# The first mixer of a two-layer encoder: values and gates follow each block, half of the output projection stands beside the last block's decays, and pools and load order are laid out anew

## The chip, the cores and the metric

One core of a Trainium2 chip runs the whole program: one launch, fp32 inputs and output in HBM. The metric is device microseconds of an execution, as a median over runs.

## The reference, cut to what matters

The program is an encoder trunk of two layers on 256 tokens of width 1024. Each layer is a token mixer and then a mixture of experts (MoE), each followed by a LayerNorm. The change touches the first mixer alone, and the order in which buffers are given to the MoE behind it.

```
q, f_fwd, f_bwd, v, gate = split(x @ w_in, 5)            # w_in 1024 x 5120
o = gated recurrence over time, forward and backward, 8 heads of 128
o = o * rsqrt(mean(o*o) + eps) * norm_w                   # by head
mix = (o * silu(gate)) @ w_out                            # w_out 1024 x 1024
x = LayerNorm(ALPHA * x + mix)
...
# MoE: top group of 4, its top 2 of 8 experts by token; 32 experts
hg, hu = split(xb @ w_up[e], 2);  y = (silu(hg) * hu) @ w_down[e]
```

All 32 experts' weights are read in both layers: 24 loads of 1 MB for a group of four experts, eight groups, 192 MB for a layer.

## The kernel before

**Weights.** Every weight comes in loads of 1 MB (`load`, line 87), issued on SyncE's (SP's) queue in the order of the program. A load is written to a slot of a ring. In the first mixer the ring is `ring1` with 9 slots (R1). For the first MoE there are 21 slots: the 9 of `ring1`, 4 of `ring2`, 5 of `ring3`, 3 of `ring4`. The last three lie in SBUF that the first mixer's own pools held. `MOE0_SLOTS` (line 34) is the order in which the first 21 loads of the MoE take slots, by ring number; it repeats after that. A load waits on SP until the last reader of what lay in its slot is done, and all loads behind it wait with it.

**Precision.** A weight is split in two fp32r parts, `whi` (ScalarE, line 265) and `wlo` (VectorE, line 266), a quarter of a load (128x512) at a time. A projection's quarter is 12 matmuls of 256 columns (`proj_w`, `proj_x`, lines 317 to 319 and 334 to 336); a quarter of the output projection is 6 matmuls of 512 columns (`out_proj`, lines 376 to 378). `Quarters` splits four quarters ahead of use.

**The first mixer, `hgrn`.** The 8 heads are four blocks b of two heads. For each block, `project(b)` (12 quarters) gives queries and forget gates; `decay(b)` makes the block's score matrix `am` in a first step (line 517) and eight levels (lines 546 and 532), each of which needs the products `kk` (line 563) and `qq` (line 566) of the level before from VectorE; `mix(b)` multiplies `am` by the values `vv` (line 594), normalises and multiplies by the gate `og`; `gate_turn(b)` (line 644) turns the result for the output projection. `values(c)` and `gated(c)` are projections of 4 quarters each. A `Side` weaves the nine steps of `decay(b)` into a stage's main work: `stage(b, quarters, main)` takes about 9 steps in that many quarters. Four stages follow `project(0)`. Then the output projection has its 16 quarters, with `mix(2)`, `mix(3)` and the preparation of the router (`routes`) between them.

**PSUM.** The levels of a decay use four banks with the tag `oa`, projections two with the tag `pj`. The output projection holds all four `oa` banks.

**The MoE.** LayerNorm statistics, the router and a gather come first; then for each group 16 loads of `w_up` (line 927) and 8 of `w_down`. The group's loads are issued as slots come free. Between the layers' MoEs stands a second mixer, a short convolution (`conv`).

Of the kernel before, what the change touches and what calls it, by code (L numbers as in the profile page):

```python
# [9 lines left out]
F32 = mybir.dt.float32  # L10
# [7 lines left out]
P = 128  # L18
D = 1024
# [11 lines left out]
FAR = 4096.0  # L31
RMS_EPS = 1e-6

MOE0_SLOTS = (2, 2, 2, 2, 1, 1, 4, 4, 4, 1, 1, 1, 3, 1, 3, 1, 1, 1, 3, 3, 3)
R1 = 9
R2 = 4
R3 = 5
# [4 lines left out]
def kernel(  # L42
# [31 lines left out]
    def bank(tag, bufs=2):  # L74
        return psum.tile([P, 512], F32, name=tag, tag=tag, bufs=bufs)
# [267 lines left out]
    def chain(*gens):  # L343
        for g in gens:
            yield from g
# [76 lines left out]
    def pools(left, name, n):  # L422
        return [left.enter_context(tc.tile_pool(name=f"{name}{k}", bufs=2, reuse_waits="tile")) for k in range(n)]
# [3 lines left out]

    def hgrn(src, left):
        w_in = hg_w_in[0]
        vam = left.enter_context(tc.tile_pool(name="vam", bufs=1))  # L430
        pm, px, pw, pj, pl = pools(left, "hg", 5)
        xtl = [p.tile([P, KD, T], F32R, name=n, bufs=1) for p, n in ((px, "xt"), (pl, "xl"))]
        rec = ExitStack()
        rc = rec.enter_context(tc.tile_pool(name="rec", bufs=2, side="right"))

        def x_evac(k2, v):
            ks = slice(2 * k2, 2 * k2 + 2)
# [2 lines left out]
        def qf(b):  # L440
            return [cols(w_in, D * z + 256 * b) for z in range(3)]

        vs = [cols(w_in, 3 * D + 256 * c) for c in range(4)]
        gs = [cols(w_in, 4 * D + 256 * c) for c in range(4)]
        order = qf(0) + vs[0:2] + qf(1) + vs[2:4] + qf(2) + gs[0:1] + qf(3) + gs[1:4]
        order += [rows(hg_w_out[0], 256 * c) for c in range(4)]
        ws = Quarters(pw, order, (0, 2, 1, 3), first=True, ahead=0,
                      between=lambda: load_x(1), lo_on=(0, 0, 0, 0))

        vv = vam.tile([P, NT, D], F32, name="vv")  # L450
        kmask = rc.tile([P, len(KINDS), P], U8, name="kmask", bufs=1)
        og = xb

# [8 lines left out]
        def project(b):  # L462
            ps = bank("pj")
            yield from proj_w(ps, xtl, ws)
            qq = rc.tile([P, 2, 2, T], F32, name="qq")
            kk = rc.tile([P, 2, 2, T], F32, name="kk")
            tt = rc.tile([P, 2, 2, T], F32, name="tt")
            QK[b] = qq, kk, tt
            th = pj.tile([P, 512], F32, name="th")
            act.activation(th, ps, AF.Tanh, scale=0.5)  # L470
            q0 = qq[:, 0].rearrange("p h t -> p (h t)")
            dve.scalar_tensor_tensor(q0, th, 1.0, ps, ALU.add, ALU.mult)
            for d in range(2):
                ps = bank("pj")
                yield from proj_w(ps, xtl, ws)
                th = pj.tile([P, 512], F32, name="th")
                act.activation(th, ps, AF.Tanh, scale=0.5)
                for h in range(2):
                    later.append((kk[:, d, h], tt[:, 1 - d, h], th[:, h * T:(h + 1) * T], 8 * d + 2 * b + h))

        ams = {}

        def firsts(kk, h):

# [7 lines left out]
        def decay(b):  # L492
            qq, kk, tt = QK[b]
            while later:
                forget()
            am = vam.tile([P, 2, NT, T], F32, name="am", bufs=4)
            ams[b] = am
            dst = am.rearrange("p hd j (k i) -> p hd j k i", k=2)

            def diag(rows_, cs):  # L500
                base = am[rows_, 0, 0, cs]
                return bass.AP(tensor=base.tensor, offset=base.offset,
                               ap=[base.ap[0], [NT * T, 2], [T + P, NT], list(base.ap[-1])])

            def scores(ps, kv):
                for hd in range(2):
                    for j in range(NT):
                        o = (hd * NT + j) * P
                        js = slice(j * P, (j + 1) * P)
                        yield ps[:, o:o + P], kv[:, hd, js], hd, js  # L510


            ks = rc.tile([P, 2, T], F32, name="ks", bufs=1)
            dve.tensor_tensor(ks, kk[:, 0], kk[:, 1], ALU.add)
            ps = bank("oa", 4)
            for o, kx, hd, js in scores(ps, ks):
                pe.matmul(o, kx, qq[:, 0, hd, js], start=True, stop=True)
            act.copy(diag(slice(0, P), slice(0, P)), ps.rearrange("p (hd j i) -> p hd j i", hd=2, j=NT))

            dve.tensor_tensor(qq[:, 1], qq[:, 0], tt[:, 1], ALU.mult)  # L520
            dve.tensor_tensor(qq[:, 0], qq[:, 0], tt[:, 0], ALU.mult)
            kc = firsts(kk, 1)
            yield

            tcur = tt
            for h in (1, 2, 4, 8, 16, 32, 64, 128):
                ps = bank("oa", 4)
                v = ps.rearrange("p (hd j i) -> p hd j i", hd=2, j=NT)
                if h == 128:
                    for hd in range(2):  # L530
                        for j in range(NT):
                            pe.matmul(v[:, hd, j], kk[:, j, hd, j * P:j * P + P],
                                      qq[:, 1 - j, hd, (1 - j) * P:(1 - j) * P + P], start=True, stop=True)
                    for j in range(NT):
                        act.copy(dst[:, :, j, 1 - j], v[:, :, j])
                    return


                def both(a, hd, o):
                    base = a[:, 0, hd, o:o + 1]  # L540
                    return bass.AP(tensor=base.tensor, offset=base.offset,
                                   ap=[base.ap[0], [2 * h, (P if hd is not None else 4 * P) // (2 * h)],
                                       [2 * T + h, 2], [1, h]])

                for o, kx, hd, js in scores(ps, kc):
                    pe.matmul(o, kx, both(qq, hd, js.start), start=True, stop=True)

                nb = T // (2 * h)

                def diagonal(a):  # L550

                    base = a[:, 0, 0, 0:1]
                    return bass.AP(tensor=base.tensor, offset=base.offset,
                                   ap=[base.ap[0], [2 * T + h, 2], [2 * h, 2 * nb], [1, h]])

                def factors(d):

                    base = tcur[:, 0, 0, 0:1]
                    o, step = (1, 4 * nb - 1) if d else (4 * nb + 1, -4 * nb - 1)
                    return bass.AP(tensor=base.tensor, offset=base.offset + o,  # L560
                                   ap=[base.ap[0], [step, 2], [2, 2 * nb], [0, h]])

                dve.tensor_tensor(diagonal(kk), diagonal(kk), factors(0), ALU.mult)
                if h < 64:
                    kc = firsts(kk, 2 * h)
                dve.tensor_tensor(diagonal(qq), diagonal(qq), factors(1), ALU.mult)
                if h < 64:
                    tn = rc.tile([P, 2, 2, nb], F32, name=f"tt{2 * h}", bufs=1)
                    tf = tcur.rearrange("p d hd (n s) -> p (d hd n) s", s=2)
                    pool.tensor_tensor(tn.rearrange("p d hd n -> p (d hd n)"), tf[:, :, 0], tf[:, :, 1], ALU.mult)  # L570
                    tcur = tn
                if h == 64:
                    for s in range(2):
                        r = slice(s * 64, s * 64 + 64)
                        act.copy(diag(r, slice(64 - s * 64, P - s * 64)), v[r, :, :, 64 - s * 64:P - s * 64])
                else:
                    dve.copy_predicated(diag(slice(0, P), slice(0, P)),
                                        kmask[:, KINDS.index(h), None, None, :].to_broadcast([P, 2, NT, P]), v)
                yield
# [95 lines left out]
            side.weave(main, after)  # L675
            side.finish()

        stage(0, 20, chain(values(0), values(1), project(1)))
        norms = load_norms()
        load_router(0)  # L680
        stage(1, 20, chain(values(2), values(3), project(2)))
        turn_norms(norms)
        stage(2, 16, chain(gated(0), project(3)), go_on((0, 6)))
        routes = router(0, lambda: pj.tile([P, 512], F32, name="th"))
        stage(3, 12, chain(gated(1), gated(2), gated(3)), go_on((1, 4), (2, 9)))
        rec.close()

        oa = [[bank("oa", 4) for f in range(2)] for t in range(NT)]
        for c in range(3):
            for _ in out_proj(oa, c, *m[c], ws):  # L690
                next(mixes[2], None)
                next(mixes[3], None)
                if c:
                    next(routes, None)
        run(routes)
        return finish_mixer(xb, src, oa, out_proj(oa, 3, *m[3], ws))

# [418 lines left out]
```

## Time and profile before

| what | value |
|---|---|
| time, median of 3 runs | 1241.23 us (1240.2 to 1242.97) |
| the profiled execution, own time | 1240.37 us |
| its span | 1238.6 us |
| busy: PE, VectorE, ScalarE, GpSimd | 976.2, 351.6, 268.1, 86.1 us |
| read from HBM | 447.05 MB |
| mean granted TensorE clock | 0.953 |

The span is the time from the first to the last instruction of the profiled execution; its own time is 1.77 us longer. A busy PE is one that has a matmul in its pipeline. The clock is a share of full speed, so 1.0 is 2.4 GHz and 0.5 is 1.2 GHz. All times inside the span count from its start.

### The profile page before, as it was taken

The numbers are of one execution on the slowest core, as the hardware profiler recorded it, in microseconds if no ns is written. First come the engines' busy times: TensorE is split into PE (matmuls) and PEld (weight loads), VectorE is DVE, ScalarE is ACT, GpSimd is POOL, SyncE is SP. The second block draws the span as 40 slices with busy tenths as digits, with TensorE's granted clock in tenths as the row PEclk, the third lists the DMA queues.
The fourth block names the chain that finished last, engine by engine and source line by source line (L and its number), as shares of the span: only waits on it lengthen the run. The fifth ranks groups of instructions, "written<-read, shape, count | busy, mean of one in ns | idle before, by whom it ended". The sixth has DMA issues, their size and how long they took to land. (4 is left out here: it accounts for less than half of the span.)

```text
span 1238.6 us, 15265 instructions
## 1 busy us (share of the span) xinstructions
PE 976.2 (79%) x6196; PEld 506.4 (41%) x6196; DVE 351.6 (28%) x602; ACT 268.1 (22%) x527; POOL 86.1 (7%) x98
## 2 busy tenths in 40 slices
PE   9999899787767676767678999879858767676875
PEld 8899897331213121222223999423213212121221
DVE  5767786310101111010103766331010101010103
ACT  5566543110101010100102554201101101010011
POOL 0110110000000000000000664000000000000001
PEclk9999999898998899998999999979998999999888
DMA  9733019999999999999999995999999999999994
GB/s 340 257 126 135 1 49 418 382 418 417 420 418 417 420 419 420 419 419 420 419 418 390 385 389 184 398 401 417 421 418 417 420 419 420 418 418 421 419 418 180
DMA packets 148304, 449.23 MB, mean 363 GB/s; under 512 B 11653, under 2 KB 44670, under 8 KB 148222
## 3 DMA queue, kind: packets, MB, share of 16 engines
q1 hardware_dynamic: 147884, 447.06, 90.5%
q8 instruction: 52, 0.85, 0.3%
q10 hardware_dynamic: 338, 1.07, 0.2%
q14 instruction: 30, 0.25, 0.1%
HBM read 447.05 MB, written 1.05 MB: 362 GB/s over the span
## 5 line engine op out<-in xcount | busy, mean ns | idle before, releaser
L927 PE MATMUL pj<-w,xg 128*32 128x512 f32 x2048 | 322.4, 629 | 92.3 <-DMA w<-in_moe_w_up_dram 92.3
L927 PE MATMUL oa<-w,hT 128*32 128x512 f32 x1024 | 173.0, 648 | 71.6 <-DMA w<-in_moe_w_down_dram 61.9
L927 PEld LDWEIGHTS pj<-w,xg 128*32 128x32 f32 x2048 | 68.2, 112 | 293.0 <-issue 162.7
L927 PEld LDWEIGHTS oa<-w,hT 128*32 128x32 f32 x1024 | 36.9, 114 | 196.1 <-DMA w<-in_moe_w_down_dram 131.9
L266 DVE TENSOR_TENSOR wlo<-w,whi 128x512 fp32r<-128x512 f32 x130 | 102.0, 800 | 50.7 <-ACT whi L265 49.7
L317 PE MATMUL pj<-xt,whi 128*128 128x256 f32 x384 | 110.7, 288 | 1.0 <-ACT whi L265 0.8
L922 ACT ACTIVATE xg<-sc,lnT 128x128 f32<-128x128 f32 x128 | 51.7, 454 | 272.1 <-PE sc L919 271.6
L319 PE MATMUL pj<-xt,wlo 128*128 128x256 f32 x384 | 109.0, 284 | 0.4 <-DVE wlo L266 0.4
L318 PE MATMUL pj<-xl,whi 128*128 128x256 f32 x384 | 108.7, 283 | 0.3 <-DVE xl L714 0.3
L265 ACT ACTIVATE whi<-w 128x512 fp32r<-128x512 f32 x160 | 98.2, 628 | 36.1 <-PE pj L318 16.7
L919 PE MATMUL sc<-oh,xb 128*128 128x128 f32 x512 | 73.4, 294 | 21.8 <-DVE oh L905 21.8
L919 PEld LDWEIGHTS sc<-oh,xb 128*128 128x128 f32 x512 | 64.1, 200 | 61.8 <-issue 38.5
L984 DVE COPY yy<-oa 128x512 f32<-128x512 f32 x14 | 9.7, 692 | 233.4 <-PE oa L927 233.4
L963 DVE SCALAR_TENSOR_TENSOR mth<-mth,pj 128x512 f32<-128x512 f32 x16 | 11.0, 688 | 224.6 <-ACT mth L962 224.6
L317 PEld LDWEIGHTS pj<-xt,whi 128*128 128x128 f32 x384 | 73.5, 191 | 1.6 <-ACT whi L265 1.0
L319 PEld LDWEIGHTS pj<-xt,wlo 128*128 128x128 f32 x384 | 73.4, 191 | 1.1 <-DVE wlo L266 1.0
L318 PEld LDWEIGHTS pj<-xl,whi 128*128 128x128 f32 x384 | 73.6, 192 | 0.6 <-DVE xl L714 0.5
L390 POOL TENSOR_SCALAR rs<-mv 128x2 f32<-128x2 f32 x4 | 0.9, 220 | 942.6 <-DVE mv L389 942.6
L943 DVE TENSOR_TENSOR oh<-oh,gate 128x256 f32<-128x256 f32 x16 | 6.8, 424 | 183.5 <-PE sc L919 183.5
L984 ACT COPY yy<-oa 128x512 f32<-128x512 f32 x14 | 8.2, 586 | 202.5 <-PE oa L927 202.5
L989 PE MATMUL oa<-yy,ogt 128*128 128x512 f32 x112 | 51.8, 606 | 0.0
L266 POOL TENSOR_TENSOR wlo<-w,whi 128x512 fp32r<-128x512 f32 x30 | 44.3, 1485 | 39.4 <-ACT whi L265 21.2
(242 smaller groups left out, 967.2 us busy)
## 6 DMA issues: line engine op xcount, KB each, us to landing
w<-in_moe_w_up_dram SPq DMA_DIRECT2D x256, 1024.0 KB, 17.8
w<-in_moe_w_down_dram SPq DMA_DIRECT2D x120, 1024.0 KB, 17.8
w<-in_hg_w_in_dram SPq DMA_DIRECT2D x19, 1024.0 KB, 9.8
w<-in_cv_w_in_dram SPq DMA_DIRECT2D x11, 1024.0 KB, 10.5
w<-in_moe_w_down_dram SPq DMA_DIRECT2D x32, 256.0 KB, 6.1
w<-in_hg_w_out_dram SPq DMA_DIRECT2D x4, 1024.0 KB, 5.0
w<-in_cv_w_out_dram SPq DMA_DIRECT2D x4, 1024.0 KB, 11.3
xa<-in_x_dram SPq DMA_DIRECT2D x4, 256.0 KB, 3.5
```

Of the source, the lines that this page charges most:

```text
L265: act.activation(hi, src, AF.Copy)
L266: (eng or dve).tensor_tensor(lo, src, hi.bitcast(F32), ALU.subtract)
L317: pe.matmul(o, hv[:, j, cs], xt[:, k], start=k == 0 and m == 0, stop=False, skip_group_check=True)
L318: pe.matmul(o, hv[:, j, cs], xl[:, k], start=False, stop=False, skip_group_check=True)
L319: pe.matmul(o, lv[:, j, cs], xt[:, k], start=False, stop=k == KD - 1, skip_group_check=True)
L919: pe.matmul(v[:, a], xs[:, t, k * P:(k + 1) * P], ohv[:, t], start=t == 0, stop=t == 1)
L922: act.activation(xg[:, k], v[:, a], AF.Identity, bias=lnb(i)[:, k:k + 1], scale=lng(i)[:, k:k + 1])
L927: pe.matmul(o[f][r], x[:, r], wv[j // 2][:, 1024 * (j % 2) + 512 * f:][:, 0:512], start=first, stop=last, tile_position=(0, 32 * j))
L943: dve.tensor_tensor(og, oh, gate[:, :, es, None].to_broadcast(sh), ALU.mult)
L963: dve.scalar_tensor_tensor(th, th, 1.0, pu[0], ALU.add, ALU.mult)
L984: evac[f](yy[:, f * 512:f * 512 + 512], py[f])
L989: pe.matmul(ps, ogt[:, t * P:(t + 1) * P], yy[:, fs], start=True, stop=True)
```

## The change

Three things change in `hgrn`, and the table of slots. First, `values(b)` and `gated(b)` of a block are projected together in stage b, ahead of `project(b+1)`; before, all values came in stages 0 and 1 and the gates in stages 2 and 3. The stages have 20, 20, 20 and 16 quarters instead of 20, 20, 16 and 12, and `mix(b)` runs in the stage after its decay from the third quarter on. Second, the output projection of blocks 0 and 1 (`out(0)`, `out(1)`, 8 quarters) stands in stage 3, beside the last decays, whose levels then use the two `pj` banks. Third, `vv` has a pool of its own, the pools `pw`, `pj`, `pl` are entered in another order, `qq`, `kk` and `tt` are in one pool for even and one for odd blocks, and `MOE0_SLOTS` is another list.

```diff
-MOE0_SLOTS = (2, 2, 2, 2, 1, 1, 4, 4, 4, 1, 1, 1, 3, 1, 3, 1, 1, 1, 3, 3, 3)
+MOE0_SLOTS = (4, 1, 1, 1, 2, 1, 1, 3, 3, 1, 1, 2, 2, 2, 1, 4, 4, 1, 3, 3, 3)
...
         vam = left.enter_context(tc.tile_pool(name="vam", bufs=1))
-        pm, px, pw, pj, pl = pools(left, "hg", 5)
+        vvp = left.enter_context(tc.tile_pool(name="vvp", bufs=1))
+        pm, px, pl, pw, pj = pools(left, "hg", 5)
...
+        rqk = [rec.enter_context(tc.tile_pool(name=f"rec{n}", bufs=1, side="right")) for n in (1, 0)][::-1]
...
-        order = qf(0) + vs[0:2] + qf(1) + vs[2:4] + qf(2) + gs[0:1] + qf(3) + gs[1:4]
+        order = qf(0)
+        for b in range(4):
+            order += vs[b:b + 1] + gs[b:b + 1] + (qf(b + 1) if b < 3 else [])
...
-        vv = vam.tile([P, NT, D], F32, name="vv")
+        vv = vvp.tile([P, NT, D], F32, name="vv")
...
+        level_banks = ["oa", 4]
...
-                ps = bank("oa", 4)
+                ps = bank(*level_banks)
...
-        stage(0, 20, chain(values(0), values(1), project(1)))
+        oa = []
+
+        def out(c):
+            if not oa:
+
+                level_banks[:] = "pj", 2
+                oa.extend([bank("oa", 4) for f in range(2)] for t in range(NT))
+            yield from out_proj(oa, c, *m[c], ws)
+
+        stage(0, 20, chain(values(0), gated(0), project(1)))
         norms = load_norms()
         load_router(0)
-        stage(1, 20, chain(values(2), values(3), project(2)))
+        stage(1, 20, chain(values(1), gated(1), project(2)), go_on((0, 2)))
         turn_norms(norms)
-        stage(2, 16, chain(gated(0), project(3)), go_on((0, 6)))
+        stage(2, 20, chain(values(2), gated(2), project(3)), go_on((1, 2)))
         routes = router(0, lambda: pj.tile([P, 512], F32, name="th"))
-        stage(3, 12, chain(gated(1), gated(2), gated(3)), go_on((1, 4), (2, 9)))
+        stage(3, 16, chain(values(3), gated(3), out(0), out(1)), go_on((2, 2)))
         rec.close()
-
-        oa = [[bank("oa", 4) for f in range(2)] for t in range(NT)]
-        for c in range(3):
-            for _ in out_proj(oa, c, *m[c], ws):
-                next(mixes[2], None)
-                next(mixes[3], None)
-                if c:
-                    next(routes, None)
+        for _ in out(2):
+            next(mixes[3], None)
+            next(routes, None)
+        run(mixes[3])
         run(routes)
```

The first place is SP's queue where the mixer's loads end and the first MoE's begin. `w_2504` and the names behind it are the MoE's first loads, in the order of `MOE0_SLOTS`; the brackets name the counters of engines (PE_49 is TensorE's) that a load waits for. Before:

```order
L87 DMA w_2293<-in_hg_w_out_dram 128x2x1024 [waits DMAHW7_49,DVE_49]
L87 DMA w_2504<-in_moe_w_up_dram 128x2x1024 [waits DVE_49,DMAHW0_49,PE_49,Activation_49]
L87 DMA w_2506<-in_moe_w_up_dram 128x2x1024 [waits DMAHW1_49,Activation_49,Pool_49]
L87 DMA w_2516<-in_moe_w_up_dram 128x2x1024 [waits DMAHW2_49]
L87 DMA w_2518<-in_moe_w_up_dram 128x2x1024 [waits DMAHW3_49]
L87 DMA w_2535<-in_moe_w_up_dram 128x2x1024 [waits DMAHW4_49]
```

Of the change, at the same place:

```order
L87 DMA w_2260<-in_hg_w_out_dram 128x2x1024 [waits DMAHW7_49,DVE_49]
L87 DMA w_2516<-in_moe_w_up_dram 128x2x1024 [waits DVE_49,DMAHW0_49,PE_49,Activation_49]
L87 DMA w_2518<-in_moe_w_up_dram 128x2x1024 [waits DMAHW1_49]
L87 DMA w_2528<-in_moe_w_up_dram 128x2x1024 [waits DMAHW2_49]
L87 DMA w_2530<-in_moe_w_up_dram 128x2x1024 [waits DMAHW3_49]
L87 DMA w_2547<-in_moe_w_up_dram 128x2x1024 [waits DMAHW4_49,Pool_49]
L87 DMA w_2549<-in_moe_w_up_dram 128x2x1024 [waits DMAHW5_49]
```

Both first loads wait for TensorE, but for another instruction. Before, the slot (of `ring2`) lies over block 3's `qq` and `kk`, and the count that the load waits for on TensorE is reached by the last level of `decay(3)` (line 532). In the change the slot (of `ring4`) lies over the `am` of blocks 0 and 3, and the count is reached by the last matmul of `mix(3)` (line 601 of the new file, 594 of the old).

The second place is TensorE's queue around these two instructions. Before, with the last level (`L532`) and then the first quarter of the output projection and `mix(3)` (`L594`):

```order
L334 MATMUL pj<-whi,xt 128x256
L335 MATMUL pj<-wlo,xt 128x256
L336 MATMUL pj<-whi,xl 128x256
L532 MATMUL oa<-qq,kk 128x128 x4
L376 MATMUL oa<-whi,mh 128x512
L377 MATMUL oa<-wlo,mh 128x512
L378 MATMUL oa<-whi,ml 128x512
L376 MATMUL oa<-whi,mh 128x512
L377 MATMUL oa<-wlo,mh 128x512
L378 MATMUL oa<-whi,ml 128x512
L594 MATMUL sc<-vv,am 128x128 x8
L376 MATMUL oa<-whi,mh 128x512
```

Of the change (`L539` is the last level, `L601` is `mix(3)`):

```order
L376 MATMUL oa<-whi,mh 128x512
L377 MATMUL oa<-wlo,mh 128x512
L378 MATMUL oa<-whi,ml 128x512
L539 MATMUL pj<-qq,kk 128x128 x4
L376 MATMUL oa<-whi,mh 128x512
L377 MATMUL oa<-wlo,mh 128x512
L378 MATMUL oa<-whi,ml 128x512
L376 MATMUL oa<-whi,mh 128x512
L377 MATMUL oa<-wlo,mh 128x512
L378 MATMUL oa<-whi,ml 128x512
L601 MATMUL sc<-vv,am 128x128 x8
L376 MATMUL oa<-whi,mh 128x512
```

What stands ahead of the last level has changed: before, quarters of a projection and no quarter of the output projection; in the change 8 quarters of the output projection, and a ninth stands between the last level and `mix(3)`.

## Rows read from the trace of the kernel before

**Rows 1.** The page's 40 slices of 31 us: share of the DMA engines, GB/s.

```profile
DMA  9733019999999999999999995999999999999994
GB/s 340 257 126 135 1 49 418 382 418 417 420 418 417 420 419 420 419 419 420 419 418 390 385 389 184 398 401 417 421 418 417 420 419 420 418 418 421 419 418 180
```

**Rows 2.** Busy time by stretch, from the span's start; the heading names the columns.

```profile
core 0: us, PE busy (x) PEld busy (x) DVE busy (x) ACT busy (x) POOL busy (x), PEclk, DMA share, GB/s
122.00:180.00 58.00, 53.84 (x443) 53.13 (x442) 46.62 (x78) 31.21 (x59) 8.52 (x14) 0.97 0.00 1
182.00:240.00 58.00, 51.58 (x323) 34.77 (x321) 30.45 (x76) 17.60 (x34) 2.51 (x4) 0.98 1.02 416
...
246.00:660.00 414.00, 301.84 (x1749) 95.34 (x1752) 45.69 (x76) 39.34 (x88) 0.00 (x0) 0.95 1.02 419
660.00:740.00 80.00, 75.10 (x522) 63.47 (x517) 50.69 (x56) 37.30 (x65) 41.60 (x32) 1.00 1.04 392
```

**Rows 3.** Groups of PE, 250 to 660 us: busy, mean ns, idle before, releaser.

```profile
L927 PE MATMUL pj<-w,xg 128*32 128x512 f32 x920 | 149.2, 630 | 46.1 <-DMA w<-in_moe_w_up_dram 46.0
L927 PE MATMUL oa<-w,hT 128*32 128x512 f32 x479 | 82.6, 649 | 40.8 <-DMA w<-in_moe_w_down_dram 36.0 <-ACT hT L969 4.7
```

**Rows 4.** Timeline of SP's queue, 90 to 262 us: start, duration of the issues.

```profile
91.55 26.35 SPq L87 DMA_DIRECT2D w<-in_hg_w_out_dram  x4
180.33 28.49 SPq L87 DMA_DIRECT2D w<-in_moe_w_up_dram  x16
```

**Rows 5.** Waits of SP's queue, 100 to 262 us: total, times, longest.

```profile
SPq L87 <- DVE qq L566: 61.2, 1, 61.2
```

**Rows 6.** Timeline of PE, 143 to 191 us: start, duration, [idle before].

```profile
144.66 1.16 PE L532 MATMUL oa<-qq,kk 128*128 128x128 f32 x8 [1.38 <-DVE qq L566]
...
179.09 1.16 PE L532 MATMUL oa<-qq,kk 128*128 128x128 f32 x8
...
180.01 0.47 PE L376 MATMUL oa<-whi,mh 128*128 128x512 f32 x1
...
181.47 1.95 PE L594 MATMUL sc<-vv,am 128*128 128x128 f32 x16
183.18 0.48 PE L376 MATMUL oa<-whi,mh 128*128 128x512 f32 x1
...
186.02 0.60 PE L644 MATMUL sc<-ident,xb 128*128 128x128 f32 x4
186.37 0.48 PE L376 MATMUL oa<-whi,mh 128*128 128x512 f32 x1
...
190.59 0.60 PE L644 MATMUL sc<-ident,xb 128*128 128x128 f32 x4
```

**Rows 7.** The same timeline, 195.3 to 220 us; the first two rows begin and end 54 matmuls.

```profile
195.37 0.48 PE L376 MATMUL oa<-whi,mh 128*128 128x512 f32 x1
...
207.50 0.39 PE L378 MATMUL oa<-whi,ml 128*128 128x512 f32 x1
207.73 1.91 PE L259 MATMUL oa<-ident,xb 128*128 128x128 f32 x16
...
219.05 3.64 PE L927 MATMUL pj<-w,xg 128*32 128x512 f32 x32
```

**Rows 8.** Waits from 0 to 260 us: total, times, longest.

```profile
PE oa L517 <- DVE ks L514: 10.4, 4, 3.0
...
PE oa L532 <- DVE qq L566: 1.4, 1, 1.4
```

**Rows 9.** Busy time by stretch again (columns as in rows 2): a slower clock.

```profile
151.00:157.00 6.00, 5.75 (x35) 5.76 (x36) 3.75 (x6) 3.08 (x5) 1.40 (x2) 0.72 0.00 0
```

**Rows 10.** Groups of VectorE, 91 to 181 us: busy, mean ns, idle before.

```profile
L266 DVE TENSOR_TENSOR wlo<-w,whi 128x512 fp32r<-128x512 f32 x37 | 25.1, 688 | 16.9 <-ACT whi L265 16.7
L566 DVE TENSOR_TENSOR qq<-qq,tt 128x512 f32<-128x512 f32 x18 | 12.5, 692 | 2.2 <-PE oa L546 2.1
L563 DVE TENSOR_TENSOR kk<-kk,tt 128x512 f32<-128x512 f32 x18 | 12.3, 685 | 0.0
L577 DVE COPY_PREDICATED am<-kmask,oa 128x512 f32<-128x512 uint8 x15 | 11.1, 738 | 0.0
```

More of the change, by code (lines that the diff above doesn't have):

```diff
@@ L464, in project @@
             yield from proj_w(ps, xtl, ws)
-            qq = rc.tile([P, 2, 2, T], F32, name="qq")
-            kk = rc.tile([P, 2, 2, T], F32, name="kk")
-            tt = rc.tile([P, 2, 2, T], F32, name="tt")
+            qq = rqk[b % 2].tile([P, 2, 2, T], F32, name="qq")
+            kk = rqk[b % 2].tile([P, 2, 2, T], F32, name="kk")
+            tt = rqk[b % 2].tile([P, 2, 2, T], F32, name="tt")
             QK[b] = qq, kk, tt
@@ L526, in decay @@
             for h in (1, 2, 4, 8, 16, 32, 64, 128):
-                ps = bank("oa", 4)
+                ps = bank(*level_banks)
                 v = ps.rearrange("p (hd j i) -> p hd j i", hd=2, j=NT)
```

## The prediction

> **What bounds the kernel now.** I began with the page's 40 slices [rows 1]. The reader is to see that the kernel has two regimes. In the first five slices the DMA engines fade out and stand still; from the slice that begins at 186 us on they are full, at 418 GB/s, with a dip to 184 GB/s around 750 us. The windows sharpen this [rows 2]: from 122 to 180 us the DMA moves nothing while PE is busy 53.84 of 58 us, so there the mixer's own work sets the pace. From 182 to 240 us the DMA moves 416 GB/s and from 246 to 660 us 419, share 1.02: the stream of the first MoE's weights has no gap left. In that stretch PE is busy 301.84 of 414 us, and the groups say what ends its waits: the loads, 46.0 us ahead of the upward matmuls and 36.0 ahead of the downward ones [rows 3]. So the end of the first MoE is the end of a stream of 192 loads, and a load of 1.05 MB at 419 GB/s takes 2.50 us: 192 of them 480 us, from about 182 to 662 us, which is where the page's DMA row leaves its level. The short convolution behind it starts when the last of these is used; from 660 to 740 us PE is busy 75.10 of 80 us, so the convolution is work of PE and keeps its length. What moves the start of the stream therefore moves everything behind it by the same amount.
>
> What starts the stream is one wait on SP's queue. The last loads of the mixer are issued from 91.55 us, the MoE's first at 180.33 us [rows 4]; between them SP waits 61.2 us in one piece, put down to `qq` of line 566 [rows 5]. The matmul that reads this `qq` (line 532, the last level of block 3) starts at 179.09 us and has left the array by 180.25 [rows 6], just before the issue. The mixer's own end is not the bound: PE leaves the output projection at 207.73 us and the experts' first matmul comes at 219.05 [rows 7], when (219.05 - 182) / 2.50 = 14.8 loads have arrived, and the first four matmul groups want four.
>
> The Trainium skill speaks of such kernels in "Trace Analysis", section Optimization Strategy: where the most contended engine changes over time, interleaving the regimes may help. By that rule the stream ought to begin deeper in the mixer; it gives no number here.
>
> **The change, part by part.** What counts is what TensorE has to do before the first load is let go. The order rows of the change show that this load now waits for the last matmul of `mix(3)`. It is at the head of SP's queue, so the other 191 wait behind it, also those whose slots (rings 1 and 2) have long been free.
>
> *Moved ahead of it on TensorE.* Eight quarters of the output projection stand beside the last decays, a ninth between the last level and `mix(3)`: 54 matmuls. 54 such matmuls lie between 195.37 and 207.73 us [rows 7]: 12.36 us. `mix(3)` itself takes 183.18 - 181.47 = 1.71 us, and the turn of block 2, which came later before, 186.37 - 186.02 = 0.35 us [rows 6]. Sum 14.4 us. The projections of values and gates are the same 32 quarters in another order, all ahead of the wait in both kernels: nothing.
>
> *Stalls that change.* Before the wait PE loses 10.4 us in four stalls at the first step of a decay, one for each block, and 1.4 us once at a last level [rows 8], at 144.66 us [rows 6], at the end of the only stage with 16 quarters. The four stay: forget gates, `ks` and the first score are chained as before, and no quarter is put between them. The 1.4 us should go, since that stage now has 20 quarters, as two stages have that show no such stall. Behind it the granted clock was 0.72 from 151 to 157 us [rows 9], a mean of the two levels 1.2 and 2.4 GHz, which cost some (1 - 0.72) x 6 = 1.7 us. It fell behind this stall and the next block's first-step stall, which follows it; I take it that without the former it does not fall, as it did not at the other first steps. Together 3.0 us less. Bounds: none of it goes (0), or all stalls go too (3.0 + 10.4 = 13.4); I take 3.0, since only these have a row that tells them from the stages without.
>
> *Two banks instead of four for the last five levels.* A bank must be read by line 577 before the level after next writes it. VectorE does `kk`, `qq` and line 577 of a level in order, so that this reading stands ahead of the next level's `qq` anyway. Work on VectorE for such a level: three operations and two splits of 0.69 to 0.74 us [rows 10], 3.5 us at most, and these overlap by some tenths; PE has two quarters, 12 x 12.36 / 54 = 2.75 us, and the level's 0.9 us (180.01 - 179.09 [rows 6]): 3.65 us. That is tight but covers it: nothing. Without cover it would be some 0.8 us for each of five levels, 4 us.
>
> *After the start.* In the change the loads 2 to 8 wait for nothing later, and 9 waits for the first quarter of `out(3)`. Eight loads keep the DMA busy for 20 us. In the kernel before, the turn of block 3 stood 190.59 - 183.18 = 7.4 us behind `mix(3)` [rows 6] with other work between; a quarter later is 9 us, so load 9 is in time. The list of slots repeats after 21 loads in both kernels, and the stream was full with either wait behind it: no gain, no loss. The chain from `mix(3)` to the turn and on to `out(3)` now has three quarters (4.1 us) to hide in where it had more, so the mixer can end some 2 us later than otherwise. This costs nothing: the experts' first matmul at about 220 us finds (220 - 194) / 2.50 = 10 loads, and needs four.
>
> *Sum.* The first issue moves from 180.33 by 14.4 - 3.0 = 11.4 us to 191.7, or by 14.4 to 194.7 if the clock and the stall stay. I take 12, nearer to the lower end. The profiled execution would go from 1240.37 to 1252.4 us; the median of the runs is 0.86 us above it, 1241.23, and so becomes **1253.2 us**, 1.0% slower.
>
> **Rivals.**
>
> 1. *The last decays stall* on two banks or on VectorE: 12 + 4 = 16 us, 1257. For it: VectorE is busy 46.62 of 58 us in that stretch [rows 2]. Against: the stage of 12 quarters, which was tighter, shows no such stall of note [rows 8]. 0.08.
> 2. *The stream catches up.* If it ran a little faster when PE trails it, part of the delay would come back. The windows differ by 416 to 419 GB/s [rows 2]; 0.7% of 480 us is 3.4 us, so 1249.8. Against: the queue was never empty before, so there is no reserve to see. 0.05. The Trainium skill, "Trace Analysis", section Roofline, puts the ceiling of a core that streams alone at about 435 GB/s for its 16 DMA engines; by that, as an estimate, 3.7% or 17.7 us could come back and the kernel would end near 1235. The trace has no long stretch above 419.
> 3. *All stalls go.* With every stall of the decays gone the issue comes at 191.7 - 10.4 = 181.3 us, 1.0 us late: 1242, no change. It needs more than 9 us of the 10.4. Against: the chain of the first step is unchanged. 0.04.
> 4. *The start of the stream doesn't decide; the mixer's end does.* Then what counts is that PE saves 3.0 us of stalls and loses about 1.1 at the end: 1.9 us faster, 1239.3, up to 3.0 (1238.2). It decides if the 21 slots are full before the experts begin. Against: only 14.8 of 21 loads had arrived by then, and 82 us of PE's waits end with a load [rows 3]. 0.05.
>
> **How the numbers follow.** The forecast has 0.78: 12 us, own range 10.5 to 15, so 1251.5 to 1256. A measurement of this kernel can tell about 0.2%, 2.5 us, from no change. Slower: the forecast and rivals 1 and 2, 0.91. Same: rival 3 and half of 4, 0.06. Faster: the rest of rival 4, 0.03. For 8 in 10 the range goes down to rival 2, 1249, and up to rival 1's edge, 1257.5.
>
> **What would show it.** In the changed kernel: SP's first load of `w_up` is issued at 191 to 195 us and put down to `mix(3)` or what feeds it; the DMA moves nothing from about 122 us until then; from then to about 673 us it shows 419 GB/s without a gap; the experts' first matmul is within 3 us of 219; the first MoE and the convolution end 12 us later than before. The saved stall shows as no wait at line 539 (the old 532) in stage 2, and a clock of 1.0 around 150 us. Wrong it would be if the stream began before 185 us, or if PE's waits for loads in the MoE shrank by the delay: then the experts' work, not the stream, would be the bound.

## The result, and the profile after

The change takes 1251.24 us (median of 4 runs, 1250.55 to 1251.66) where the kernel before took 1241.27 beside it (4 runs): a ratio of 1.0078, interval 1.0061 to 1.0096. It is slower by 10 us. 1253.2 was forecast: the measured time lies 0.3 us below the forecast's own range (1251.5 to 1256) and inside the wider one (1249 to 1257.5). The profiled execution has a span of 1248.8 us and a time of its own of 1250.55, 10.18 more than before.

I read the profile of the change in the order of the prediction. First the page's slices (31 us each), which answer to [rows 1]:

```profile
DMA  9733008999999999999999995999999999999995
GB/s 337 252 126 129 8 1 329 419 384 419 420 421 416 421 419 419 420 420 420 420 419 390 390 412 187 362 410 420 419 421 417 420 420 419 420 419 420 420 419 182
```

The fifth and the sixth slice are now empty, and the full level is reached one slice later. The busy time by stretch (columns as in rows 2) sharpens it:

```profile
122.00:192.00 70.00, 67.45 (x508) 65.00 (x506) 56.33 (x92) 37.78 (x71) 14.00 (x15) 0.98 0.05 16
194.00:240.00 46.00, 37.99 (x249) 22.35 (x248) 21.70 (x61) 10.85 (x23) 2.50 (x4) 0.95 1.02 416
...
246.00:670.00 424.00, 309.74 (x1737) 93.41 (x1736) 44.81 (x72) 39.34 (x88) 0.00 (x0) 0.94 1.02 417
670.00:750.00 80.00, 74.81 (x517) 62.25 (x518) 50.09 (x55) 37.14 (x65) 40.12 (x29) 1.00 1.05 394
```

PE is busy for 67.45 of the 70 us in which little more than the mixer's last load arrives (16 GB/s are 1.1 MB); then the stream runs at the rate that it had before, without a gap, and ends later. SP's queue shows the start (start, duration, issues):

```profile
94.43 27.01 SPq L87 DMA_DIRECT2D w<-in_hg_w_out_dram  x4
192.28 28.35 SPq L87 DMA_DIRECT2D w<-in_moe_w_up_dram  x16
```

The first load is issued at 192.28 us, 11.95 later than in [rows 4]. The waits of that queue (total, times, longest) say what held it; they answer to [rows 5]:

```profile
SPq L87 <- DVE am L584: 63.6, 1, 63.6
...
SPq L87 <- PE sc L601: 7.2, 1, 7.2
```

The two waits stand one behind the other, ahead of the first load: SP looks at VectorE's counter first, then at TensorE's. From 121.44 us (94.43 + 27.01) the first takes it to 185.0, when VectorE has written the last `am` that it asked for, and the second, 7.2 us for `mix(3)` (line 601), to the issue. In the kernel before 61.2 us for `qq` and 1.2 for the last level (`SPq L87 <- PE oa L532: 1.2, 1, 1.2`) made up the time in the same way. Whoever reads the long row alone names the wrong work. PE's timeline (start, duration):

```profile
187.99 1.06 PE L539 MATMUL pj<-qq,kk 128*128 128x128 f32 x8
...
190.25 1.95 PE L601 MATMUL sc<-vv,am 128*128 128x128 f32 x16
191.96 0.48 PE L376 MATMUL oa<-whi,mh 128*128 128x512 f32 x1
...
206.06 1.91 PE L259 MATMUL oa<-ident,xb 128*128 128x128 f32 x16
...
217.38 3.21 PE L939 MATMUL pj<-w,xg 128*32 128x512 f32 x28
```

The 16 matmuls of `mix(3)` leave the array at 192.20 us, 0.08 before the issue. The mixer itself ends at 206.06 us, 1.67 *earlier* than in [rows 7], and the experts begin 1.67 us earlier. So the mixer became faster and the kernel slower. The groups of PE from 258 to 670 us answer to [rows 3]:

```profile
L939 PE MATMUL pj<-w,xg 128*32 128x512 f32 x896 | 152.4, 633 | 56.6 <-DMA w<-in_moe_w_up_dram 56.5
L939 PE MATMUL oa<-w,hT 128*32 128x512 f32 x432 | 80.4, 691 | 33.1 <-DMA w<-in_moe_w_down_dram 29.1 <-ACT hT L981 4.0
```

PE waits 85.6 us for loads where it waited 82.0: the experts still stand behind the stream. The end of the first MoE has moved by 11.51 us (the first matmul of line 1007, 1019 in the change, among its last downward ones, starts at 677.22 us instead of 665.71).

### The profile page after: what moved, and what is told of

Read it like the earlier page. It is cut to its first block, busy times and chain, and to the rows that moved or that the text cites. A ratio compares the mean times of both kernels' runs of the same rounds, so it can differ in the third digit from the quotient of the medians.

```text
span 1248.8 us, 15270 instructions
## 1 busy us (share of the span) xinstructions
PE 986.0 (79%) x6196; PEld 504.4 (40%) x6196; DVE 349.5 (28%) x602; ACT 267.8 (21%) x527; POOL 90.2 (7%) x98
## 3 DMA queue, kind: packets, MB, share of 16 engines
HBM read 447.05 MB, written 1.05 MB: 359 GB/s over the span
## 5 line engine op out<-in xcount | busy, mean ns | idle before, releaser
L939 PE MATMUL pj<-w,xg 128*32 128x512 f32 x2048 | 328.9, 631 | 104.3 <-DMA w<-in_moe_w_up_dram 104.2
L939 PE MATMUL oa<-w,hT 128*32 128x512 f32 x1024 | 177.6, 676 | 63.4 <-DMA w<-in_moe_w_down_dram 54.0
L939 PEld LDWEIGHTS oa<-w,hT 128*32 128x32 f32 x1024 | 35.9, 115 | 192.7 <-DMA w<-in_moe_w_down_dram 125.7
L931 PEld LDWEIGHTS sc<-oh,xb 128*128 128x128 f32 x512 | 62.9, 197 | 60.9 <-issue 37.6
## 6 DMA issues: line engine op xcount, KB each, us to landing
w<-in_hg_w_in_dram SPq DMA_DIRECT2D x19, 1024.0 KB, 10.1
```

The costliest lines, as they stand in the source:

```text
L931: pe.matmul(v[:, a], xs[:, t, k * P:(k + 1) * P], ohv[:, t], start=t == 0, stop=t == 1)
L939: pe.matmul(o[f][r], x[:, r], wv[j // 2][:, 1024 * (j % 2) + 512 * f:][:, 0:512], start=first, stop=last, tile_position=(0, 32 * j))
```

## The experiments

The account to be tested, T1 in what follows: the time is set by when SP's queue lets the first load go. That is set by where the *first* slot's last reader stands on TensorE, and by all that TensorE does, or loses, ahead of that reader. So the order of work and the list of slots each have a price of their own, and the two add. Where some loads go ahead of the wait, T1 counts the data moved by the time from which the stream runs without a gap. The rivals put the loss on the order of work alone, on the layout alone, or let the start of the stream count only in part; each expectation says which it weighs.

**1. `order_only`: the order of the change on the pools and the list of before.** The first slot then waits for the last level of block 3 again.

```diff
-MOE0_SLOTS = (4, 1, 1, 1, 2, 1, 1, 3, 3, 1, 1, 2, 2, 2, 1, 4, 4, 1, 3, 3, 3)
+MOE0_SLOTS = (2, 2, 2, 2, 1, 1, 4, 4, 4, 1, 1, 1, 3, 1, 3, 1, 1, 1, 3, 3, 3)
...
-        pm, px, pl, pw, pj = pools(left, "hg", 5)
+        pm, px, pw, pj, pl = pools(left, "hg", 5)
...
-        vv = vvp.tile([P, NT, D], F32, name="vv")
+        vv = vam.tile([P, NT, D], F32, name="vv")
```

> The changed kernel's order of work, with the pools and the slot list of the kernel before. The first load of the MoE then waits for the last level of block 3 (line 539 of the change), which ended at about 188.9 us in the changed kernel's trace, and no longer for the mix of block 3 at 192.0. Theory 1 (the time follows the issue of the first load one for one): issue at about 189.1 instead of 192.3, so 3.1 us less than the change, 1248.1 us, 6.8 above the kernel before. Theory 2 (the new order costs by itself, through TensorE's clock or waits, and the slot list costs nothing): as the change, 1251.2. Theory 3 (the wait at the head of the load queue costs only by the slot list, the order nothing): as the kernel before, 1241.3.

Measured: 1248.86 us (6 runs) against 1241.45 (23 runs of before, shared by runs 1 to 4), 1.0064 [1.0044, 1.0083]; first issue 191.87 us, where T1 had 189.1. The order alone costs most of it, and an account by the layout alone is out. What the layout adds can't be told from this one: its interval holds both. The clock was 0.69 from 35 to 40 us and 0.56 from 160 to 165 in this profile, so its mixer ran later than that of the change (it ended at 208.80 us instead of 206.06).

**2. `layout_only`: the order of before on the pools and the list of the change** (the other half of the diff undone). The first slot waits for `mix(3)`, which stands where it stood.

> The order of work of the kernel before, with the pools and the slot list of the change. The first load waits for the mix of block 3, which ends at about 183.3 us in the trace of before, 3.1 us behind the last level. Theory 1: issue at 183.5 instead of 180.3, 3.2 us more than before, 1244.4 us. Theory 2 (order alone costs): as before, 1241.3. Theory 3 (slot list alone costs): the whole of the change, 1251.

Measured: 1243.63 us (12 runs), 1.0020 [1.0007, 1.0033]; first issue 185.15 us, and `mix(3)` leaves PE at 183.13 + 1.95 = 185.08. So the layout has a price too, some 2 us, which agrees with T1's 1244.4. The issue came 4.82 us later than before, not 3.2: in this execution the whole mixer ran 1.67 us later (its end 209.40 for 207.73). The two prices add, as T1 has it: 0.64% and 0.20% make 0.84%, and the change measured 0.78% beside its own runs of before.

**3. `one_first`: the change, with three free slots ahead of the one that waits for `mix(3)`.**

```diff
-MOE0_SLOTS = (4, 1, 1, 1, 2, 1, 1, 3, 3, 1, 1, 2, 2, 2, 1, 4, 4, 1, 3, 3, 3)
+MOE0_SLOTS = (1, 1, 1, 4, 2, 1, 1, 3, 3, 1, 1, 2, 2, 2, 1, 4, 4, 1, 3, 3, 3)
```

> The change with one entry of its slot list moved: the slot that waits for the mix of block 3 is fourth instead of first, behind three slots of ring 1. Those three loads wait only for the splits of block 3's projection and go out at about 135 to 145 us, while the DMA engines stand still; the fourth waits as the first did. Theory 1 (what counts is the data moved by the time the stream runs without a gap): three loads of 2.50 us less, 7.5 us below the change, 1243.7 us. Theory 2: the order of the mixer's work is untouched, so as the change, 1251.2. A third possibility, that early loads only fill slots which then stand full until the experts begin: also 1251.

Measured: 1243.12 us (12 runs), 1.0014 [0.9999, 1.0030]; T1 said 1243.7. The waits for `am` and `mix(3)` are still there (41.5 and 7.2 us) but three loads of 2.50 us have gone ahead of them, from 129.72 us on. Nothing on TensorE was touched, and 8 of the 10 us are back.

**4. `free_first`: the change, with the list in the order in which slots fall free.**

```diff
-MOE0_SLOTS = (4, 1, 1, 1, 2, 1, 1, 3, 3, 1, 1, 2, 2, 2, 1, 4, 4, 1, 3, 3, 3)
+MOE0_SLOTS = (1, 1, 1, 1, 2, 1, 3, 1, 1, 2, 2, 2, 1, 4, 4, 4, 1, 3, 3, 3, 3)
```

> The change with its slot list sorted by the time at which the slots fall free in the trace of the change: four of ring 1, one of ring 2, one of ring 1, one of ring 3, two of ring 1, and so on. Nine loads then wait for something that is over by about 182 us, the tenth for the last level of block 3 at about 188. Theory 1: nine loads of 2.50 us are out of the way and the rest starts 4.4 us earlier, 26.9 us less than the change, 1224.4 us. If the slots are full before the experts begin (21 loads would have landed at about 220 us, and the experts begin at 217.4), some 2 us of it are lost, 1226. Theory 2: 1251.2, since the order of the mixer's work is untouched. If the first expert groups' work becomes the bound instead of the loads, anything between 1226 and 1240.

Measured: 1228.58 us (4 runs), 0.9892 [0.9876, 0.9909]. The sign and most of the size are T1's; it said 1224.4 to 1226, 2.6 to 4.2 us less. The waits of SP's queue in this kernel, and the busy time around the experts' first matmul at 219.81 us (the last number is GB/s):

```profile
SPq L87 <- DVE wlo L266: 79.9, 11, 13.2
SPq L87 <- PE pj L939: 25.4, 6, 12.4
...
196.00:222.00 26.00, 23.36 (x158) 17.56 (x160) 15.22 (x43) 8.66 (x16) 2.50 (x4) 1.00 1.02 417
222.00:224.00 2.00, 2.00 (x21) 0.86 (x14) 0.00 (x0) 0.00 (x0) 0.00 (x0) 1.00 0.87 299
224.00:226.00 2.00, 2.00 (x21) 0.90 (x24) 0.00 (x0) 0.81 (x2) 0.00 (x0) 1.00 0.99 373
```

No wait is longer than 13.2 us, and the second row is new: all 21 slots are given out, and SP waits for the experts' own matmuls (line 939) to free one. But a wait of the queue is not yet a wait of the stream. The loads issued before keep the DMA at 417 GB/s up to 222 us, and it falls below 420 for 4 us only, an estimated loss of 0.8 us. For the rest, this mixer ended 2.4 us later than that of the change (the clock was 0.66 from 35 to 40 us and 0.83 from 115 to 125), and with it the moment at which the list's last slots fall free; some 1 us of T1's 4.2 stays open.

**5. `old_free_first`: the kernel before, with a list made in the same way.** Runs 5 to 7 were made beside 9 runs of before of 1243.3 us.

```diff
-MOE0_SLOTS = (2, 2, 2, 2, 1, 1, 4, 4, 4, 1, 1, 1, 3, 1, 3, 1, 1, 1, 3, 3, 3)
+MOE0_SLOTS = (1, 1, 1, 1, 1, 2, 2, 2, 2, 4, 4, 4, 3, 1, 3, 1, 1, 1, 3, 3, 3)
```

> The kernel before, with its slot list sorted by the time at which its slots fall free: five of ring 1, four of ring 2, three of ring 4 and so on. Five loads then wait only for splits of projections, over by about 166 us; the sixth waits for the last level of block 3, as the first did. Theory 1 (data moved before the stream runs without a gap): five loads of 2.50 us, 12.5 us less than before, 1228.9 us. If the gain of the sorted list on the changed kernel came only with the new order of work: 1241.4.

Measured: 1230.96 us (4 runs), 0.9894 [0.9874, 0.9914], as expected (0.9899). With the list in order, the order of work before and that of the change are alike (0.9894 and 0.9892): what the change did to the projections is worth next to nothing by itself.

**6. `change_gap`: the change, with one more step in the decay, between the product `ks` and the matmul that reads it**, so that a quarter of the stage's main work hides the wait of the first step.

```diff
             dve.tensor_tensor(ks, kk[:, 0], kk[:, 1], ALU.add)
+            yield
             ps = bank(*level_banks)
...
-            side = Side(decay(b), 9, quarters, 0, forget)
+            side = Side(decay(b), 10, quarters, 0, forget)
```

> The change, with the first step of each decay cut in two: the sum ks in one step, its matmul in the next, so that quarters of a projection stand between them; ten steps instead of nine in a stage. In the trace of the change TensorE waits 9.2 us for ks in four places, and after the last of them the granted clock was 0.76 from 157 to 163 us, worth 1.4 us. Theory 1: all of this lies before the wait of the first load, so the stream starts 9.2 to 10.6 us earlier, and the time is 1240.6 to 1242.0 us. If stalls of TensorE in the mixer are not what holds the start (VectorE's chain is, and the stall moves to another level): between 1247 and 1251.

Measured: 1233.14 us (5 runs), 0.9915 [0.9899, 0.9932]. This is a miss: twice the gain that was forecast. The waits of SP's queue in this kernel:

```profile
SPq L87 <- DVE am L585: 25.8, 1, 25.8
SPq L87 <- DVE ss L608: 24.5, 2, 24.1
...
SPq L87 <- PE sc L602: 11.7, 1, 11.7
```

and its busy time by stretch (the last number is GB/s):

```profile
160.00:170.00 10.00, 8.57 (x58) 7.73 (x57) 9.87 (x19) 4.48 (x9) 1.22 (x4) 1.00 1.03 420
170.00:180.00 10.00, 10.00 (x57) 8.41 (x56) 9.82 (x16) 5.31 (x11) 0.00 (x0) 1.00 0.40 164
180.00:190.00 10.00, 9.07 (x55) 7.73 (x54) 7.21 (x11) 4.20 (x9) 1.57 (x2) 1.00 0.00 0
190.00:200.00 10.00, 8.87 (x47) 6.77 (x46) 7.22 (x15) 1.44 (x3) 0.00 (x0) 1.00 0.45 171
```

The stream starts at 152 us, moves eight loads, stands still again and resumes near 196. The extra step changed what the first load waits for: no longer `mix(3)` but `mix(2)`. So the first slot must lie over another `am` now, that of block 2; the addresses themselves no row shows. PE's `mix(2)` leaves at 149.97 + 1.95 = 151.92 us, just before the issue (the 11.7 us of line 602). The ninth load then waits 24.1 us. Eight loads are 20 us. So two causes were mixed in this run, and it says nothing clean about the stalls.

**7. `free_gap`: `free_first` with the step of run 6.**

> The change with the sorted slot list and with the decays' first step cut in two. Theory 1: 9.2 us less than with the sorted list alone, 1219.4 us, since the tenth load waits for the last level of block 3, which comes that much earlier, and the experts begin as much earlier too. If the 21 slots are full before the experts begin, some 2 to 4 us of it are lost: 1221.5 to 1223.5. If the stalls only move to other levels: 1226 to 1228.6.

Measured: 1216.91 us (5 runs), 0.9791 [0.9774, 0.9809]: 2.1% faster than before, and the fastest of all. T1's 1219.4, a ratio of 0.982, lies outside the interval: this too gained more than T1 said. PE's waits of the decays in it, where the change has 9.2 us at the first steps (`PE oa L524 <- DVE ks L521: 9.2, 4, 3.0`):

```profile
PE oa L554 <- ACT kc L494: 1.4, 1, 1.4
...
PE oa L525 <- DVE ks L521: 1.1, 1, 1.1
```

The clock was 1.00 from 120 to 210 us, and the mixer ended 10.1 us earlier than in `free_first`, for 11.7 us of span. T1 had only the 9.2 us of stalls; the slow stretches of `free_first`, which this execution lacks, would make up the rest, but that is argued and not shown.

**8 and 9. `old_gap` and `order_gap`: the same step in the kernel before, and in `order_only`.** These are the clean form of run 6: in both, the slots' addresses and the instruction that the first one waits for stay as they were, so only the stalls change. They were run beside 13 runs of before of 1242.5 us.

```diff
             dve.tensor_tensor(ks, kk[:, 0], kk[:, 1], ALU.add)
+            yield
             ps = bank("oa", 4)
...
-            side = Side(decay(b), 9, quarters, 0, forget)
+            side = Side(decay(b), 10, quarters, 0, forget)
```

> The kernel before, with one step between the product ks and the matmul that reads it, so that a piece of the stage's main work stands there on TensorE (the decay has ten steps instead of nine). The list, the pools and the instruction that the first slot waits for (the last level of block 3) stay as they were, so that here nothing but the stalls changes. T1, what TensorE loses ahead of that wait is carried to the end one to one: of the 10.4 us at the first steps some 1 us stays, as in the change with the same step, the 1.4 us at one last level may stay; the slow clock at 151 to 157 us (1.7 us) goes. The first load is issued at 168 to 171 us instead of 180.33, and the time is 10 to 12 us shorter: a ratio of 0.990 to 0.992. T2, the start of the stream is carried only in part (the stream is not the bound throughout): a ratio of 0.995 or above. T3, the start of the stream decides nothing: 0.999 to 1.001.

> The same step put into order_only (the order of the change on the pools and the list of before). The first slot waits for the last level of block 3 as in order_only, so nothing but the stalls changes. T1: order_only issued its first load at 191.87 us with 9.2 us of first-step stalls and two stretches of a slow clock (0.69 and 0.56 over 5 us each, some 3.7 us); with some 1 us of stalls left and a full clock the issue comes at 179.5 to 184 us, 8 to 12 us earlier, and the ratio to the kernel before is 1.0064 less 0.0064 to 0.0097: 0.997 to 1.000. T2, carried in part: above 1.002. T3: 1.000 for every such kernel, which order_only's 1.0064 already contradicts.

Measured: `old_gap` 1232.4 us (4 runs), 0.9922 [0.9905, 0.9938]; `order_gap` 1240.43 us (10 runs), 0.9986 [0.9974, 0.9998]. PE's waits in `old_gap`, to be held against [rows 8]:

```profile
PE oa L518 <- DVE ks L514: 2.3, 2, 1.2
...
PE oa L547 <- ACT kc L487: 1.2, 1, 1.2
PE oa L533 <- DVE qq L567: 1.2, 1, 1.2
```

The 11.8 us of [rows 8] have become 4.7; the first issue came at 172.40 us, 7.93 earlier (168 to 171 was expected: 1.2 us of a new wait at line 547 and 1.3 more at `ks` stand in between). In `order_gap` it came at 181.46, 10.41 earlier than in `order_only`. Both intervals overlap what T1 gave (0.990 to 0.992 and 0.997 to 1.000), and neither reaches T2's (0.995 and 1.002).

**The runs together.** "Issue" is the first load of `w_up`, "experts" the first matmul of the first MoE, both in the profiled execution; the differences are taken from its span. "Loads" is what has landed of the first MoE's loads by 280 us: the GB/s from 130 us (128 in `one_first`, 120 in `free_gap`, in each behind the mixer's last load) to 280 us, at 1.05 MB a load. From 280 to 640 us the stream moves 419 or 420 GB/s in all eleven kernels.

| kernel | issue | experts | loads | span | span - issue | span - experts | span + 2.50 x loads |
|---|---|---|---|---|---|---|---|
| before | 180.33 | 219.05 | 37.9 | 1238.6 | 1058.3 | 1019.5 | 1333.3 |
| the change | 192.28 | 217.38 | 33.3 | 1248.8 | 1056.5 | 1031.4 | 1332.0 |
| order_only | 191.87 | 220.12 | 33.5 | 1249.0 | 1057.1 | 1028.9 | 1332.8 |
| layout_only | 185.15 | 220.73 | 35.9 | 1241.1 | 1056.0 | 1020.4 | 1330.8 |
| old_gap | 172.40 | 211.15 | 41.3 | 1228.4 | 1056.0 | 1017.3 | 1331.7 |
| order_gap | 181.46 | 209.71 | 37.6 | 1239.0 | 1057.5 | 1029.3 | 1333.0 |
| one_first | 129.72 | 216.71 | 36.7 | 1239.2 | 1109.5 | 1022.5 | 1331.0 |
| change_gap | 152.00 | 209.71 | 40.6 | 1229.0 | 1077.0 | 1019.3 | 1330.5 |
| free_first | 132.85 | 219.81 | 42.5 | 1226.8 | 1094.0 | 1007.0 | 1333.0 |
| old_free_first | 134.37 | 225.01 | 40.5 | 1229.7 | 1095.3 | 1004.7 | 1331.0 |
| free_gap | 123.79 | 209.72 | 46.7 | 1215.1 | 1091.3 | 1005.4 | 1331.8 |

In the six kernels whose stream starts in one piece behind one wait, the span is the first issue and 1056.0 to 1058.3 us, whatever the order, the layout or the moment at which the experts begin (209.71 to 220.73). In the five that start early in pieces the first issue says little. There the loads count, and they do so in all eleven: the span and 2.50 us for each load landed by 280 us make 1330.5 to 1333.3, while the spans differ by 33.9 us.

In the three kernels with a sorted list the span is also the experts' first matmul and 1004.7 to 1007.0. That looks like a second bound, 21 slots that stand full until the experts begin. The rates speak against it: up to the experts' first matmul the DMA of these three moves 416 to 421 GB/s (from 196, 200 and 188 us on), and only some 20 loads have landed by then (in `free_first` 232 GB/s over 89.8 us). The last slots of a sorted list fall free with the mixer's tail, so that in these kernels the stream and the experts move together. A stream that began earlier still would meet that bound next, since the last of the 21 slots is then being filled; no run shows it.

## Why the prediction was right

*What bounds the kernel.* Right, and the table is its best test. The experts' first matmul was 1.67 us earlier in the change and was worth nothing. By the Trainium skill, "Perfetto Trace Analysis", section Optimization Strategy, interleaving regimes that differ in their most contended engine may improve performance; these traces agree, since the two sorted lists, which let loads into the empty stretch, gave 1.1% each (`free_first`, `old_free_first`).

*What moves ahead of the wait.* 14.4 us was the forecast for 54 matmuls, `mix(3)` and a turn. The nine quarters stand there, and the first issue follows `mix(3)` by 0.08 us. The forecast for that issue was 191.7 to 194.7 us with 12 us as the step; it came after 11.95.

*What is saved.* Of the 3.0 us, the 1.4 at a last level came: PE has no wait at line 539 in the mixer. The 1.7 us of the slow clock did not come as argued. I took it that the clock would not fall without that stall; it fell all the same, at the same first step, that of block 3, around a stall of 2.55 us as before. The clock of 1.00 from 143 to 151 us, which was to be the sign, shows only that this step ends its stall 5.79 us later now (157.04 for 151.25). Behind it:

```profile
157.00:163.00 6.00, 5.96 (x40) 5.96 (x41) 1.98 (x3) 2.09 (x4) 0.00 (x0) 0.76 0.01 3
```

That is (1 - 0.76) x 6 = 1.4 us against 1.7. In its place the four first steps lost 9.2 instead of 10.4 us, which I had put at no change. So 1.4 + 1.2 + 0.3 = 2.9 us were saved where 3.0 were forecast, from other sources than I named: this term held by luck. One thing no term had: in this execution the first projection began 0.67 us later (8.01 for 7.34). 14.4 - 2.9 + 0.7 makes 12.2, for the 11.95 measured.

*Two banks.* Right: no wait for a bank or for VectorE appears in stage 3, and rival 1 is out.

*After the start.* Right: from the first issue to 262 us no wait of SP's queue is longer than 2.5 us, the ninth load's included, and the DMA shows no gap after 194 us but the dip behind the router's loads, which both kernels have. The tail of the mixer has stalls of 0.93, 0.30 and 0.78 us, where the kernel before had 0.88 and 0.74: 0.4 us more, not the 2 that were argued (1.1 in rival 4). They cost nothing here.

*The size at the end.* The profiled execution lost 10.18 us where the start lost 11.95. Up to the first MoE's end 11.51 us were still there; the conv began 11.62 later; of that 10.85 us were left at the second MoE's first group, and 10.2 at the end. What gave them back stays open. It is the one place where the sum is off: the step at the start came as forecast, and carrying it to the end one for one was 2 us too much. The six kernels in one piece scatter by 2.3 us in span - issue, with the kernel before at the upper end, so it may be no more than that of single executions; the medians differ by 9.97.

*The rivals.* 3 (all stalls go) is out by the 9.2 us. 2 (the stream catches up) is out: 416 and 417 GB/s where it had 416 and 419; and the ceiling of about 435 GB/s that the Trainium skill gives in "Perfetto Trace Analysis", section Roofline, no run here reaches: from 280 to 640 us none is above 420. 4 (the mixer's end decides) is out for the change: the mixer's end came 1.67 us earlier, and the kernel is 10 us slower. Its condition, 21 slots full of landed loads before the experts begin, was reached in no run; `free_first`, `old_free_first` and `free_gap` come close to it, with some 20 loads landed.

## What to carry to other kernels

A queue that issues in order starts when its *first* entry may go, so a list of buffers has to be sorted by the moment at which each falls free in the program as it now runs, and looked at again after every reordering (or any new step that rotates a pool): here one misplaced entry held back slots that were free for some 60 us (the first load went at 129.72 us in `one_first`, at 192.28 in the change). Ahead of such a release, work and stalls of the releasing engine are carried to the end about one to one (10.41 us of issue were 10.0 of span from `order_only` to `order_gap`), and behind it, as long as the stream has no gap, they cost nothing. To know which of two ends decides, subtract each candidate's moment from the span in several variants, or count what has landed by a fixed moment: the one that decides leaves a constant in all of them. A constant in some of them can come from two things that move together, and the rate of the stream tells which it is.

## What the runs showed of the hardware

The granted clock is not the same in two executions of alike code. Behind a first-step stall of 2.58 us that ended at 113.11 us of the kernel before it stayed at 1.00; around one of 2.55 us that ended at 157.04 us of the change it fell (0.50 from 157 to 159 us). Behind the first such stall, 3.04 to 3.05 us in seven kernels, it was 1.00 from 35 to 40 us in three (before, the change, `one_first`) and 0.66 to 0.72 in the four others (`order_only`, `layout_only`, `free_first`, `old_free_first`). The mixers of `free_first` and of the change do the same work in the same order; the former has two slow stretches that the latter has not, 3.4 us by (1 - 0.66) x 5 + (1 - 0.83) x 10, and ends 2.4 us later.

The 128 KB of the second of the router's loads took SP's queue 9.44 or 9.45 us to issue in eight of the kernels, 4.25 to 4.83 us in the three with a sorted list, and 1.94 us at 28 us of the kernel before. By the rates some 4 loads of weights were still on their way at that moment in the change, some 2 in `free_first` (an estimate); whether that is the cause was not tried. In the change the DMA moved 257 GB/s behind it, from 253 to 260 us, where it had moved 420 from 240 to 253:

```profile
243.00 9.44 SPq L222 DMA_DIRECT2D wr<-in_moe_w_expert_dram  x1
```

All kernels here have this dip, so it takes no part in their differences, and it was not tried for itself.
